# Turning an encoder's input with two engines and widening its first group of products, in one fused float32 kernel

## The chip, the cores and the metric

The kernel runs on one core of a Trainium2 chip. The metric is the device time of one execution in microseconds (us); the figure given for a kernel is the median of its runs. An engine is called by its name or by the profile's short form: TensorE (PE, with PEld for its weight loads), VectorE (DVE), ScalarE (ACT), GpSimd (POOL) and SyncE (SP, which here only issues transfers).

## What is computed

One layer of an encoder, for 256 prompt rows and 32 sample rows of 2048 features, all in float32. The change is in the first two lines; the rest follows them.

```python
xn   = rmsnorm(x, norm_mix_pre)              # x * rsqrt(mean(x*x) + eps) * g
proj = xn @ w_in                             # 2048 -> 5664 columns: u_pool 1024 | z 2048 | xBC 2560 | dt 32
pool = pool_mixer(u_pool)                    # trailing means, then a small product per group
ssd  = ssd_mixer(z, xBC, dt)                 # causal conv, chunked scan, gate, grouped norm
x    = x + rmsnorm(concat[pool, ssd] @ w_out, norm_mix_post)
x    = x + rmsnorm(conv_ffn(rmsnorm(x, norm_ffn_pre)), norm_ffn_post)
```

The new histories and states of the pooling, the convolutions and the scan are outputs too.

## The kernel before

**Tiles.** The 256 + 32 rows are the 288 columns of every product. A tile is 128 features by 288 rows; `xn` has 16 of them (`KD`). Weights stand still in TensorE, 128x128 at a time, and the tile streams past. A float32 product is made of three: each operand is split into a high half and a rest (`hi`, `lo`, type float32r), and `mm3` (L163 to L165) adds hi·hi, hi·lo and lo·hi into one accumulator. ScalarE copies the high half (`whi`, L146; `xn`, L120) and VectorE subtracts (`wlo`, L147; `xn`, L121).

**Projections.** `project` computes some output tiles of 128 columns each over all 16 feature tiles. `fetch_w` loads weights on SP's queue into four buffers (`raw`), `split_w` splits them, and the products accumulate in one of five PSUM banks (`acc_ps`). Three more banks (`aux_ps`) serve everything else. A scheduler in the compiler orders each engine's instructions by priority and its own estimate of time; what goes through `tc.keep_in_program_order` stays in the order of the source.

**The start.** The input arrives with rows on the partitions and has to be turned, features on the partitions. The first call of `project` computes four output tiles (B and C of the scan, 256 columns each) and a narrow one (dt, 32 columns, both halves side by side, `split_narrow`, L158 and L159, products L185 and L186): 16 x 4 x 3 + 32 = 224 products. Its hook `input_tiles` loads 2 or 4 feature tiles, and TensorE turns each of them with three transposes into an auxiliary bank (L299, L300, L301); ScalarE and VectorE split the result into `xn`, with the norm's gain as a scale, and VectorE copies it unscaled (`xT`, L304) for a later residual sum. ACT's queue stores `xT` to DRAM. The last hook first turns the other parameters (`columns`, L281; `ptf`, L325).

**The sums of squares.** Behind the group, ScalarE squares the untransposed rows in three instructions (L348, L349). The square root (L351) and the reciprocal are taken on 128x3 numbers, TensorE spreads them over the partitions (L355), and a copy (L359) makes `rstd`, 128x288. Every eviction of a projection multiplies by `rstd` (`conv_in`, L380 and L381, into one of four `ebuf` buffers).

**What follows.** The next projections are eight pairs of xs tiles (96 products each), then z, the pooling input, w_out and the feed-forward weights. Between them VectorE works on the convolutions, the dt chain and the scan's masks, and TensorE multiplies quads of heads (`ssd_quad`, `py`, L562 to L568). SP's queue carries weights, blocks of transposed tiles (`blocks_out`, whose tile has one buffer) and reads of what was stored.

**Other instructions that the steps below use.** VectorE's copy at L239 repeats a small selector from SBUF to SBUF; GpSimd clears four buffers at L245; L618 is the reciprocal of another norm, on 128x288, and `psum_t` (L611) its sum on TensorE.

Of the kernel before, what the change touches and what calls it, by code (L numbers as in the profile page):

```python
# [8 lines left out]
F32 = mybir.dt.float32  # L9
# [32 lines left out]
TAIL = NT - P  # L42


@with_exitstack
def body(
# [79 lines left out]
    ahead = [0]  # L126

    def fetch_w(view, kb, nk, c0, nc_):
        raw = wpool.tile([P, nk, nc_], F32, tag="raw", name="raw")
        with tc.high_priority(offset=ahead[0]):  # L130
            sp.dma_start(out=raw, in_=view[:, kb : kb + nk, c0 : c0 + nc_])
        return raw
# [18 lines left out]
    def split_narrow(raw, kb, nk, nc_, after):  # L151

        both = xin.tile([P, nk, 2, nc_], F32R, tag="both", bufs=2, name="both")
        with ExitStack() as order:
            order.enter_context(tc.high_priority(offset=ahead[0]))
            for ins in after:
                order.enter_context(tc.issue_after(ins.ins))
            act.activation(both[:, :, 0, :], raw, AF.Copy)  # L158
            dve.tensor_tensor(both[:, :, 1, :], raw, both[:, :, 0, :].bitcast(F32), op=ALU.subtract)  # L159
        return [(kb + k, both[:, k, :, :].rearrange("p r c -> p (r c)")) for k in range(nk)]  # L160

    def mm3(out, wh, wl, a, start, stop):
        pe.matmul(out, wh, a[:, 0, :], start=start, stop=False)  # L163
        pe.matmul(out, wh, a[:, 1, :], start=False, stop=False)  # L164
        pe.matmul(out, wl, a[:, 0, :], start=False, stop=stop)  # L165

    def project(view, groups, acts, ksplit, before=None, done=None, spare=(), hold=(), behind=None):
# [7 lines left out]
        for i, (kb, n) in enumerate(ksplit):  # L175
# [5 lines left out]
            for raw, (c0, w) in zip(raws, groups):  # L181
                if w < P:
                    for k, both in split_narrow(raw, kb, n, w, after or ()):
                        o = accs[m0][: 2 * w, :]
                        pe.matmul(o, both, acts[k][:, 0, :], start=k == k_first, stop=False)  # L185
                        pe.matmul(o, both, acts[k][:, 1, :], start=False, stop=k == k_last)  # L186
                    continue
                parts = split_w(raw, kb, n, w, ((after or ()) if m0 else ()) + (hold if i else ()))
# [24 lines left out]

    ident = const.tile([P, P], F32, name="ident")
    make_identity(nc, ident)
    ones = const.tile([P, P], F32, name="ones")
    pool.memset(ones, 1.0)
# [7 lines left out]
    tc.keep_in_program_order(act.activation(warm, eps_t, AF.Copy))  # L225
# [22 lines left out]
    start = ExitStack()  # L248
    xin = start.enter_context(tc.tile_pool(name="xin", bufs=1))

    g0_in = xin.tile([KD, P], F32, name="g0_in")
    act.dma_start(out=g0_in, in_=rows(norm_mix_pre))
# [5 lines left out]
    xt = xin.tile([P, 2, D_MODEL], F32, name="xt")  # L258
    xs_ = xin.tile([NS, D_MODEL], F32, name="xs_")
    xpv = x_prompt.rearrange("o (b p) d -> p (o b) d", p=P)  # L260
# [17 lines left out]
    def columns(src, n, name):  # L278
        o = const.tile([P, n], F32, name=name)
        p_ = aux([P, n], "pt")  # L280
        pe.transpose(p_, src, ident[:n, :n])  # L281
        dve.tensor_copy(o, p_)
        return o

    g_mix_pre = columns(g0_in, KD, "g0")


    xn = []
    xT = xin.tile([P, KD, NT], F32, name="xT")
    xT_d = dram.tile([P, KD, NT], F32, name="xT_d")  # L290

    def input_tiles(kb, n):
        c = slice(kb * P, (kb + n) * P)
        sp.dma_start(out=xt[:, :, c], in_=xpv[:, :, c])
        sp.dma_start(out=xs_[:, c], in_=x_sample[0][:, c])
        for t in range(kb, kb + n):
            p_ = aux([P, NT], "pt")
            c = slice(t * P, (t + 1) * P)
            pe.transpose(p_[:, 0:P], xt[:, 0, c], ident)  # L299
            pe.transpose(p_[:, P:NP_], xt[:, 1, c], ident)  # L300
            pe.transpose(p_[:, NP_:NT], xs_[:, c], ident[:NS, :NS])  # L301
            a = atile("xn")
            last = split_from(a, p_, g_mix_pre[:, t : t + 1])
            dve.tensor_copy(xT[:, t, :], p_)  # L304
            xn.append(a)
        act.dma_start(out=xT_d[:, kb : kb + n, :], in_=xT[:, kb : kb + n, :])
        return last

    def parameters():
        pb = columns(pb_in, 108, "pb")  # L310
        g_mix_post = pb[:, 60:76]
        g_ffn_pre = pb[:, 76:92]
        g_ffn_post = pb[:, 92:108]
        pa = columns(pa_in, 124, "pa")
        pah = const.tile([P, 100], F32, name="pah")
        act.activation(pah, pa[:, 0:100], AF.Copy, scale=0.5)
        p_scale = pa[:, 100:108]
        g_ssd = const.tile([P, NX], F32, name="g_ssd")
        act.activation(g_ssd, pa[:, 108:124], AF.Copy, scale=0.5)
        pc = columns(pc_in, 120, "pc")  # L320
        pf = const.tile([P, 6, NF * 2], F32, name="pf")
        for i in range(0, 6, 3):
            p_ = aux([P, 3, NF * 2], "ptf")
            for j in range(3):
                pe.transpose(p_[:, j, :], pf_in[:, i + j, :], ident[: NF * 2, : NF * 2])  # L325
# [896 lines left out]
```

## Time and profile before

| what | value |
|---|---|
| median of 3 runs | 1353.92 us (1353.91 to 1354.41) |
| the profiled execution's own time | 1354.27 us |
| its span, first to last instruction | 1352.6 us |
| TensorE's mean granted clock | 0.999 |
| bytes moved | 252.13 MB, 186 GB/s over the span |

The span is 1.67 us shorter than the execution's own time, which holds what lies around it. A group of instructions is told by line, engine, operation and tile, with the busy time and the mean duration; "start us, us" in a timeline are start and duration from the span's beginning, and matmuls overlap, so that the distance of two starts says more than a duration. In a table of waits the columns after the colon are the total, the number and the longest. In brackets stands how long the engine was idle just before an instruction, and what ended it. VectorE is busy 38.9 of the first 57 us, and 30.8, 30.1, 31.3 and 28.7 us in the stretches from 68, 101, 135 and 169 us (33 or 34 us each).

### The profile page before, as it was taken

How to read it: one execution, taken by the hardware profiler on the slowest of the kernel's cores; microseconds unless marked ns; L12 is line 12 of the kernel's file. 1: busy time of each engine (PE TensorE's matmuls, PEld its weight loads, DVE VectorE, ACT ScalarE, POOL GpSimd, SP SyncE). 2: the span in 40 equal slices, each digit the busy share in tenths (PEclk: the TensorE clock that was granted, in tenths of full speed). 3: DMA queues.
4: the chain of work that ended last, by engine and by line, in shares of the span. 5: the costliest groups of instructions: out<-in, count | busy, mean ns of one | idle time of the engine just before them, and what ended most of it. 6: DMA issues, size and time to landing. Idle time of an engine off the chain costs nothing.

```text
span 1352.6 us, 25723 instructions
## 1 busy us (share of the span) xinstructions
PE 1340.1 (99%) x10199; PEld 1327.7 (98%) x10199; DVE 886.6 (66%) x1519; ACT 669.5 (50%) x1003; POOL 233.2 (17%) x394
## 2 busy tenths in 40 slices
PE   8999999999999999999999999999999999999997
PEld 7999999999999999999999999999999999999997
DVE  6898988779644479977676644335666666664454
ACT  6557767446534455645444433334444444454443
POOL 3132112222223320211121100001111111101110
PEclk9999999999999999999999999999999999999999
DMA  8869985464756546876545545554554554576663
GB/s 269 250 192 280 257 249 167 154 221 151 243 179 201 159 132 191 239 196 182 183 156 163 173 144 169 172 179 156 175 168 156 175 169 156 170 232 181 191 182 94
DMA packets 300135, 252.13 MB, mean 186 GB/s; under 512 B 75728, under 2 KB 293050, under 8 KB 299886
## 3 DMA queue, kind: packets, MB, share of 16 engines
q1 hardware_dynamic: 296942, 243.46, 59.0%
q0 software_dynamic: 2320, 4.65, 1.2%
q10 hardware_dynamic: 752, 2.37, 0.5%
q8 instruction: 80, 1.31, 0.4%
q14 instruction: 41, 0.34, 0.1%
HBM read 236.13 MB, written 14.31 MB: 185 GB/s over the span
## 4 chain that ended last, share of the span: by engine, by line
PE 99%; DVE 0%; DMA 0%; ACT 0%; issue 0%; DVEq 0%
PE acc L163 31%; PE acc L165 31%; PE acc L164 31%; PE pst L852 1%; PE py L562 1%; PE acc L1128 1%; PE acc_x L164 0%; PE acc_x L163 0%; PE acc_x L165 0%; PE py L564 0%; DMA xt<-in_x_prompt 0%; PE pt L299 0%; PE acc L1129 0%; PE pt L301 0%; DVE wlo L147 0%; PE acc L186 0%
## 5 line engine op out<-in xcount | busy, mean ns | idle before, releaser
L147 DVE TENSOR_TENSOR wlo<-raw,whi 128x1024 fp32r<-128x1024 f32 (+1 forms) x416 | 493.3, 1188 | 347.9 <-ACT whi L146 346.6
L146 ACT ACTIVATE whi<-raw 128x1024 fp32r<-128x1024 f32 (+1 forms) x416 | 426.6, 1028 | 498.0 <-PE acc L164 421.0
L163 PE MATMUL acc<-hn,whi 128*128 128x288 f32 x1376 | 404.1, 295 | 0.0
L164 PE MATMUL acc<-hn,whi 128*128 128x288 f32 x1376 | 403.6, 294 | 0.3 <-DVE hn L911 0.3
L165 PE MATMUL acc<-hn,wlo 128*128 128x288 f32 x1376 | 403.1, 294 | 0.0
L164 PEld LDWEIGHTS acc<-hn,whi 128*128 128x128 f32 x1376 | 259.7, 189 | 0.7 <-DVE hn L911 0.7
L165 PEld LDWEIGHTS acc<-hn,wlo 128*128 128x128 f32 x1376 | 259.6, 189 | 0.0
L163 PEld LDWEIGHTS acc<-hn,whi 128*128 128x128 f32 x1376 | 257.2, 187 | 0.1
L163 PE MATMUL acc<-xn,whi 128*128 128x288 f32 x704 | 209.3, 299 | 0.0
L164 PE MATMUL acc<-xn,whi 128*128 128x288 f32 x704 | 208.0, 296 | 0.0
L165 PE MATMUL acc<-xn,wlo 128*128 128x288 f32 x704 | 207.2, 296 | 0.0
L163 PE MATMUL acc<-fa,whi 128*128 128x288 f32 x682 | 201.9, 296 | 0.0
L164 PE MATMUL acc<-fa,whi 128*128 128x288 f32 x682 | 201.9, 296 | 0.0
L165 PE MATMUL acc<-fa,wlo 128*128 128x288 f32 x682 | 201.5, 295 | 0.0
L164 PEld LDWEIGHTS acc<-xn,whi 128*128 128x128 f32 x704 | 133.6, 190 | 0.3
L165 PEld LDWEIGHTS acc<-xn,wlo 128*128 128x128 f32 x704 | 132.9, 189 | 0.3
L163 PEld LDWEIGHTS acc<-xn,whi 128*128 128x128 f32 x704 | 132.4, 189 | 0.5
L164 PEld LDWEIGHTS acc<-fa,whi 128*128 128x128 f32 x682 | 128.6, 188 | 0.0
L163 PEld LDWEIGHTS acc<-fa,whi 128*128 128x128 f32 x682 | 128.1, 188 | 0.0
L165 PEld LDWEIGHTS acc<-fa,wlo 128*128 128x128 f32 x682 | 127.9, 188 | 0.0
L945 POOL COPY fc_stage<-ebuf 128x4 f32<-128x4 f32 x88 | 27.8, 316 | 503.6 <-DVE ebuf L944 460.2
L951 DVE SCALAR_TENSOR_TENSOR fc<-ebuf,pf,fc 128x290 f32<-128x290 f32 x176 | 90.4, 517 | 3.1 <-ACT fc L949 0.5
(341 smaller groups left out, 1660.7 us busy)
## 6 DMA issues: line engine op xcount, KB each, us to landing
raw<-in_w_up SPq DMA_DIRECT2D x80, 1024.0 KB, 5.2
raw<-in_w_in SPq DMA_DIRECT2D x40, 1024.0 KB, 5.7
raw<-in_w_down SPq DMA_DIRECT2D x32, 1024.0 KB, 5.3
raw<-in_w_out SPq DMA_DIRECT2D x24, 1024.0 KB, 5.6
raw<-in_w_down SPq DMA_DIRECT2D x16, 768.0 KB, 5.0
raw<-in_w_up SPq DMA_DIRECT2D x14, 512.0 KB, 4.1
gb<-g_d SPq DMA_DIRECT2D x8, 832.0 KB, 5.4
raw<-in_w_in SPq DMA_DIRECT2D x6, 512.0 KB, 6.0
```

The source lines that it names most:

```text
L146: act.activation(hi, raw[:, k : k + n, :], AF.Copy)
L147: dve.tensor_tensor(lo, raw[:, k : k + n, :], hi.bitcast(F32), op=ALU.subtract)
L163: pe.matmul(out, wh, a[:, 0, :], start=start, stop=False)
L164: pe.matmul(out, wh, a[:, 1, :], start=False, stop=False)
L165: pe.matmul(out, wl, a[:, 0, :], start=False, stop=stop)
L562: ins = pe.matmul(y[c, 0:256], xw[:, 0, f_], m[:, h, 0:256], start=True, stop=False)
L852: ins = pe.matmul(st[:, o, :], x_, btok[:, gi, b, :], start=b != 1, stop=b != 0)
L945: pool.tensor_copy(fc_stage[:, :, :, i], e[:, 256:324].rearrange("p (s c) -> p s c", c=34)[:, :, 0:2])
L951: dve.scalar_tensor_tensor(c, e[:, r_ : r_ + 290], pf[:, r_, i : i + 1], c, op0=ALU.mult, op1=ALU.add)
L1128: pin(pe.matmul(o, hi, f2[k][:, :, c], start=k == 0, stop=end, skip_group_check=True))
```

## The change

The first group now computes six output tiles and dt: the four of B and C and the first pair of xs, whose own call of `project` goes (the pair's banks are two of the three auxiliary ones). It runs over ten chunks of features: four of one tile, six of two. The first four tiles (512 features) are still turned by TensorE, from a load of their own (`x0`, `x0s`), and the turn of the next one is placed at the tenth product of a chunk. The other twelve are loaded so that each group of 32 partitions holds another 128 features of 32 rows, and VectorE transposes them in blocks of 32. For that, features beyond 512 go to partitions in fours (`p j`), in the weights' rows, the gain and the stored `xT` alike; `fetch_w` reads `w_in` in two transfers. Fifteen dummy products (`keep_busy`) are put before the real ones; their operand `busy` is made by three VectorE copies of `ones`. Squares are taken chunk by chunk on ScalarE; GpSimd and TensorE bring them together, and root and reciprocal are now taken on 128x288. The parameters' PSUM copies go from VectorE to ScalarE, `xT`'s stores from ACT's queue to SP's, one per tile, behind the second xs pair's loads. Nearly all of the group is pinned in program order.

```diff
+CHUNKS = ((0, 1), (1, 1), (2, 1), (3, 1), (4, 2), (6, 2), (8, 2), (10, 2), (12, 2), (14, 2))
+BUSY = 10
...
+            if len(view.shape) == 4:
+                for k in range(kb, kb + nk, 4):
+                    src = view[:, k // 4] if k else win0
+                    sp.dma_start(out=raw[:, k - kb : k - kb + 4, :], in_=src[:, :, c0 : c0 + nc_])
...
+    busy = xin.tile([P, NT], F32R, name="busy")
+    for o, n in BLK:
+        pin(dve.tensor_copy(busy[:, o : o + n], ones[:, 0:n]))
...
+    win = w_in.rearrange("o (c p j) w -> p (o c) j w", p=P, j=4)
+    win0 = w_in[0, 0 : 4 * P, :].rearrange("(k p) w -> p k w", p=P)
...
+    def input_load(c):
+        for i in range(4):
+            pin(sp.dma_start(out=xt[NS * i : NS * (i + 1), 0:8, c - 1, :], in_=xpv[i][:, :, c, :]))
+
+    def first_load(kb, n):
+
+        raw = wpool.tile([P, n, NW], F32, tag="raw", name="raw")
+        src = win0[:, kb : kb + n] if kb < 4 else win[:, kb // 4, kb % 4 : kb % 4 + n]
+        pin(sp.dma_start(out=raw[:, :, 2 * P :], in_=src[:, :, O_B : O_B + NW - 2 * P]))
+        pin(sp.dma_start(out=raw[:, :, : 2 * P], in_=src[:, :, O_X : O_X + 2 * P]))
+        raws.append(raw)
...
+    pin(act.dma_start(out=g_in, in_=norm_mix_pre[0, 0 : 4 * P].rearrange("(k p) -> k p", p=P)))
+    first_input(sp, 0, 0)
+    first_input(act, 1, 0)
+    pin(act.dma_start(out=x0s, in_=x_sample[0, :, 0 : 4 * P]))
+    first_load(*CHUNKS[0])
+    first_input(sp, 0, 1)
+    first_input(sp, 1, 1)
+    first_load(*CHUNKS[1])
+    first_load(*CHUNKS[2])
+    first_load(*CHUNKS[3])
+    input_load(1)
...
-    def input_tiles(kb, n):
-        c = slice(kb * P, (kb + n) * P)
-        sp.dma_start(out=xt[:, :, c], in_=xpv[:, :, c])
-        sp.dma_start(out=xs_[:, c], in_=x_sample[0][:, c])
-        for t in range(kb, kb + n):
...
-        act.dma_start(out=xT_d[:, kb : kb + n, :], in_=xT[:, kb : kb + n, :])
...
+    first = [aux([P, NT], "acc_x") for _ in range(2)]
+    first += [acc_ps.tile([P, NT], F32, tag="acc", name="acc") for _ in range(5)]
+
+    def keep_busy(n):
+
+        for _ in range(n):
+            pin(pe.matmul(first[1], busy[:, 0:P], busy, start=True, stop=True))
+
+    keep_busy(BUSY)
...
+    def turn_first(t):
+        p_ = aux([P, NT], "pt")
+        for b in range(2):
+            pin(pe.transpose(p_[:, b * P : (b + 1) * P], x0[:, b, t * P : (t + 1) * P], ident))
+        pin(pe.transpose(p_[:, NP_:], x0s[:, t * P : (t + 1) * P], ident[:NS, :NS]))
+        return p_
+
+    def prepare(i, p_=None):
...
+        w = xin.tile([P, n, 2 * NW + HEADS], F32R, tag="w", bufs=3, name="w")
...
+        if i == 0:
+            pin(act.activation(xn[0][:, 0, :], p_, AF.Copy, scale=g_mix_pre[:, 0:1]))
+        for c in pieces:
+            pin(act.activation(hi[:, :, c], raw[:, :, c], AF.Copy))
+        pin(act.activation(w[:, :, 2 * NW :], raw[:, :, NB:], AF.Copy))
+        for t in tiles:
+            if p_ is None:
+                pin(dve.transpose(
+                    xT[t].rearrange("p (b t) -> p b t", t=NS),
+                    xt[:, :, t // 4 - 1, :].rearrange("p b (f j) -> p b f j", j=4)[:, :, :, t % 4],
+                ))
...
+        if p_ is None:
+            for c in pieces:
+                pin(dve.tensor_tensor(lo[:, :, c], raw[:, :, c], hi[:, :, c].bitcast(F32), op=ALU.subtract))
+        for t in tiles:
+            pin(dve.scalar_tensor_tensor(
+                xn[t][:, 1, :], xT[t] if p_ is None else p_, g_mix_pre[:, t : t + 1], xn[t][:, 0, :].bitcast(F32),
+                op0=ALU.mult, op1=ALU.subtract,
+            ))
+        if p_ is not None:
+            pin(dve.tensor_copy(xT[kb], p_))
+            for c in pieces:
+                pin(dve.tensor_tensor(lo[:, :, c], raw[:, :, c], hi[:, :, c].bitcast(F32), op=ALU.subtract))
+        if i + 4 < len(CHUNKS):
+            first_load(*CHUNKS[i + 4])
...
+    p_ = turn_first(0)
+    keep_busy(5)
+    ahead_w = [prepare(0, p_)]
+    for i, (kb, n) in enumerate(CHUNKS):
+        if 4 <= i + 1 < len(CHUNKS):
+            ahead_w.append(prepare(i + 1))
...
+        if i == len(CHUNKS) - 1:
+
+            pool.tensor_tensor(
+                spots, ssum[:, :9].unsqueeze(2).broadcast_to([P, 9, NS]), sel4.unsqueeze(1).broadcast_to([P, 9, NS]),
+                op=ALU.mult,
+            )
...
+            last_split[:] = [
+                pin(act.activation(rstd, p_, AF.Sqrt, bias=eps_t, scale=1.0 / D_MODEL)),
+                pin(dve.reciprocal(rstd, rstd)),
+            ]
+        w = ahead_w.pop(0)
+
+        products = [
+            (r, m, k, x) for m in (2, 3, 4, 5, 0, 1) for k in range(n) for r, x in ((0, 0), (0, 1), (1, 0))
+        ]
+        if i == 0:
+            products.sort(key=lambda q: (q[0], q[3]))
+        products += [(None, 6, k, x) for k in range(n) for x in range(2)]
+        for q, (r, m, k, x) in enumerate(products):
+            if q == 10 and i < 3:
+                ahead_w.append(prepare(i + 1, turn_first(i + 1)))
...
+    xs_ps = [first[:2], project(win, [(O_X + 256, 256)], xn, K16, wait=last_split)]
+    xT_f = xT_d.rearrange("c p j n -> (c p j) n")
+    for t in range(KD):
+        pin(sp.dma_start(out=xT_d[t // 4, :, t % 4, :] if t > 3 else xT_f[t * P : (t + 1) * P, :], in_=xT[t]))
```

Here `NB` is 768 and `NW` 800 columns, the six tiles and dt.

231 lines of the change are left out of this document (128 added, 103 removed).

## The prediction

> **What bounds the kernel now.** I read the page's busy times first. TensorE has work for 99% of the span, so the time is the sum of its instructions and its waits, and an edit counts only by what it takes from or adds to that line.
>
> ```profile
> PE 1340.1 (99%) x10199; PEld 1327.7 (98%) x10199; DVE 886.6 (66%) x1519; ACT 669.5 (50%) x1003; POOL 233.2 (17%) x394
> ```
>
> TensorE's waits come next: 5.2 of the 6.6 us lie before 7 us; none lies between 42 and 300 us.
>
> ```profile
> PE pt L281 <- DMA g_in<-in_norm_mix_pre: 3.4, 1, 3.4
> PE pt L299 <- DVE xT L304: 1.5, 1, 1.5
> PE psum_f L1050 <- ACT fsq L1173: 1.1, 1, 1.1
> ```
>
> Then TensorE's timeline: start, duration, line. A product is issued each 0.24 us until 12.4 us, and each 0.132 us later (37 between 57.04 and 61.93). The clock column shows 1.00 in both stretches, so I take the clock from this spacing. A turned input tile is a hole: from 24.37 to 25.09 there are three transposes and one product, 0.59 us more than the product. Other holes cost 0.54 to 0.59; I use 0.58.
>
> ```profile
> 4.02 0.48 PE L299 MATMUL pt<-ident,xt 128*128 128x128 f32 x1 [0.34 <-DMA xt<-in_x_prompt]
> ...
> 7.27 0.83 PE L163 MATMUL acc<-xn,whi 128*128 128x288 f32 x2
> ...
> 10.17 0.68 PE L163 MATMUL acc<-xn,whi 128*128 128x288 f32 x2
> ...
> 24.37 0.27 PE L299 MATMUL pt<-ident,xt 128*128 128x128 f32 x1
> 24.48 0.27 PE L300 MATMUL pt<-ident,xt 128*128 128x128 f32 x1
> 24.68 0.24 PE L301 MATMUL pt<-ident,xs__137 32*128 32x32 f32 x1
> 24.86 0.40 PE L163 MATMUL acc<-xn,whi 128*128 128x288 f32 x1
> ```
>
> **The yardstick.** The new first group computes 320 products: the old group's 224 and the 96 of the first xs pair. I compare when these 320 are issued. Before: the first 28 are out at 14.24 us; 292 x 0.132 = 38.5; eleven tiles still to turn, 6.4; the end of one more, 0.2; parameter transposes (0.11 + 0.11 + 0.39 + 0.27), 0.9; L355, 0.95. Sum **61.2 us**. As a check, 180 products stand ahead of L355, which gives 41.8; the trace has it at 41.95.
>
> **After, step by step.** The last operand sets each step, so I read the loads' arrivals from ACT's timeline (the bracket tells what ended ACT's idle time).
>
> ```profile
> 6.09 0.63 ACT L146 ACTIVATE whi<-raw 128x512 fp32r<-128x512 f32 x1 [0.18 <-DMA raw<-in_w_in]
> ...
> 7.70 0.63 ACT L146 ACTIVATE whi<-raw 128x512 fp32r<-128x512 f32 x1 [0.59 <-DMA raw<-in_w_in]
> ...
> 10.62 0.63 ACT L146 ACTIVATE whi<-raw 128x512 fp32r<-128x512 f32 x1 [0.44 <-DMA raw<-in_w_in]
> ```
>
> By the kernel's sizes, 550, 1060 and 1900 KB were queued up to these three loads.
>
> *First product.* Chunk 0's first weight piece ends at 590 KB: about 6.0 us. ACT copies 544 columns in 0.65, so the first product is at 6.7 (7.27 before). The fifteen added dummy products lie where TensorE waits for loads; ones' memset ends at 1.02, three VectorE copies of some 0.2 each make the dummy operand by 1.7, and ten products at 0.24 end at 4.1, where the first input lands. If the clock is up by 8 us the chunk's 20 products end at 9.9.
>
> *Chunk 1.* Its weights end at 1380 KB: 8.8 us between the rows of 7.70 and 10.62, which are also the bounds. ACT: 800 columns 0.85, dt columns 0.15, split 0.45: 10.3. DVE in its pinned order: low half 0.43, copy 0.37, then the weights' low half (800 columns, 0.98 between the 0.69 of 512 and the 1.21 of 1024), with 0.1 of handovers: **12.2 us**. Chunk 1's third product needs that. A chunk 0 still at half speed is mostly hidden in this wait; it would move it to 12.4.
>
> *Chunks 2 and 3.* The tile is turned at the tenth product of the chunk before, and one auxiliary bank is left for it. From the turn: 0.55 + 0.5 (ACT) + 0.43 + 0.37 + 0.98 + 0.2 handovers = 3.03. TensorE meanwhile has 0.58 + 12 x 0.132 = 2.16. Wait 0.85 each.
>
> *Chunk 4.* VectorE starts its blocks after chunk 3's low half: two transposes (0.39 start to start in the blocks rows), 1600 columns 1.75, low half 0.43, handover 0.1: 3.1 against 2.5 of products. Wait 0.6. The trace has no strided block transpose: at nothing more than a plain row, or twice it, this wait is 0.6 to 1.4; I take 0.6, the same element count.
>
> *Chunks 5 to 9.* VectorE needs 0.78 + 1.75 + 0.86 = 3.4 per chunk, ACT 2.6 (4.0 with three squares), TensorE 40 x 0.132 = 5.3. A chunk brings 1.1 MB (weights 820 KB, input 290), 208 GB/s over 5.3 us; the first two slices of the page moved 269 and 250. So block transposes, squares, input loads and SP's extra issues (0.45 us each, 39 of them, 17.6 us of the 57) lie under products; if loads fell to 200 GB/s they would cost 0.2 us per chunk. The 16 stores of xT (7.2 us of issue) move from ACT's queue to SP's, between weight loads that go out a buffer release, some 10 us, ahead of use; their tiles are done, so they hold nothing up.
>
> *End of the group.* Parameters 0.9; sums 0.48 (a 288-column psum_t) + 0.95 (as L355) = 1.4. Then the new wait: the next product needs a bank, since all five accumulators are taken. The reciprocal is now on 128x288 and the rows price it:
>
> ```profile
> L618 DVE RECIPROCAL rg<-rg 128x288 f32<-128x288 f32 x2 | 3.9, 1948 | 0.6 <-ACT rg L617 0.6
> ```
>
> Behind it on VectorE stand two weight halves (2 x 1.1) and the evictions. From the sums' end: 0.55 + 1.95 + 2.2 + 0.34 + 0.34 + 0.2 = 5.6, against 5.3 of products: wait 0.4. ACT's table load lies ahead of the sums. POOL's product for the sums (1.1 to 1.4 us by its 128x288 rows) has a chunk of cover.
>
> Sum: 12.2 + 298 x 0.132 (39.3) + two turns 1.2 + 1.7 + 0.6 + 0.9 + 1.4 + 0.4 = **57.7 us**, a gain of 3.5. From some 290 us on every compute engine's order in the changed build is as before, so I carry the gain through. Profiled execution: 1354.27 (span 1352.6 and 1.67 around it) - 3.5 = 1350.8; the median of the runs shown, 1353.92, is 0.35 lower: **1350.4**.
>
> **Rivals.**
>
> *A. The dummy operand is late (1351.9).* The dummy products need VectorE copies from SBUF to SBUF, pinned ahead of all else on TensorE. The trace has one such copy beside GpSimd work:
>
> ```profile
> 1.80 2.08 DVE L239 COPY sel<-sel 32x128 f32<-32x128 f32 x1
> ```
>
> ```profile
> 2.52 1.28 POOL L245 MEMSET ebuf<- 128x326 f32 x4
> ```
>
> 128 columns take 2.08 us and end with the last memset (3.80). If the three new copies wait likewise, dummies run from 4.25 to 6.7, the turn ends at 7.6, the split and weights give a first product at 8.85, chunk 1's low half comes at 13.3 to 14.1: 1.1 to 1.9 lost, 1351.9 in the middle. Against it, and why I don't take it as likeliest: GpSimd pauses at 1.23, just after the new copies are asked for at 1.05 (ones' memset ends at 1.02 in the new order), where the old copy came at 1.80 into an unbroken row of memsets. *SBUF — State Buffer* (the Trainium skill, Who interferes with whom) says that a Vector copy in a two-port mode and a GpSimd operation exclude one another for a whole instruction; the copy row agrees, and by that rule this rival holds.
>
> *B. VectorE's backlog (1358.1).* Before, VectorE has done 42.7 us of work when the 320 products are out; after, about 33 (four turned tiles at 1.7, twelve others at 0.83 with 10.5 for their weights, reciprocal 1.95, two weight halves 2.2, start 1.5). So 9.7 us move behind them, where VectorE idles 14.0 us between 68 and 203, 8 of them in order behind stores. If less than 6.2 us of the idle is usable the gain is gone; with 2 usable the kernel is 4.2 slower. Against it: ACT waited there for weight buffers, so the splits ran ahead.
>
> *C. Chunk 1's weights land at the later row (1352.2).* 10.6 instead of 8.8: 1.8 less gain, since the chain behind them stays. For it: each transfer is queued behind the input. Against it: fewer bytes stand ahead than at that row.
>
> *D. The small waits shrink (1348.0).* Chunk 1 lands at the earlier row, 1.1 sooner, and half of the waits of 1.7 + 0.6 + 0.4 is covered, 1.35: 2.4 more. For it: weight packets of 2176 bytes replace 1024. Against it: VectorE's chain per chunk is as long either way.
>
> *TensorE: Matmul & The Clock Gate* (the Trainium skill, Part 1) states a busy window of 3.4 us before full speed, free-running. By it the dummies would raise the clock between 5 and 8.5 us; the spacing row, 5.4 us after 6.96, allows that. The sum by 12.4 us instead is 0.2 worse.
>
> **How the numbers follow.** What can be told from no change is 0.2%, 2.7 us: faster is under 1351.2, slower over 1356.6. Forecast 0.40 (0.36 of it faster), A 0.24 (0.04 faster), B 0.16 (0.12 slower), C 0.08 (same), D 0.12 (faster). Faster 0.52, same 0.36, slower 0.12. The range holds forecast, A, C and D and leaves out B: from D, 1348.0, to A's dear end (1.9) with the dear strided transpose (0.8) and slow loads (1.0), 1354.1.
>
> **What would show it.** First product near 6.7, or near 8.9 with the first dummy after 4 us (A). Waits for the weights' low half in chunks 1 to 3, near 12.2 and twice 0.85. One wait of the product after the group on VectorE's eviction. No TensorE wait between 60 and 300 us, or B. Wrong altogether if chunks 5 to 9 wait for loads, or if the spacing after 13 us isn't 0.132.

## The result, and the profile after

The changed kernel takes **1359.05 us** (median of 11 runs, 1355.02 to 1362.12) where the kernel before takes 1353.93 (11 runs beside it, 1353.36 to 1354.49): a ratio of 1.0034, 95% interval 1.0022 to 1.0046. It is 0.34% slower, outside the range and on the other side of the forecast. The profiled execution is one of the longer ones: 1361.21 us, a span of 1359.3, against 1354.27 and 1352.6 before. So 6.9 us are to be found in the traces, and 5.1 in the medians.

The first line of the changed kernel's page, busy times and instructions:

```profile
PE 1342.0 (99%) x10180; PEld 1328.6 (98%) x10180; DVE 889.6 (65%) x1509; ACT 672.6 (49%) x1028; POOL 235.4 (17%) x395
```

VectorE as a whole does 3.0 us more than before; nothing here tells of trouble. TensorE's table of waits does:

```profile
PE psum_t L740 <- POOL gsum L762: 3.8, 1, 3.8
PE acc L475 <- DVE w L397: 1.9, 3, 0.6
PE acc_x L337 <- DVE busy L213: 1.7, 1, 1.7
PE acc L164 <- DVE wlo L157: 1.6, 3, 0.8
```

The second and third lines lie in the start and were forecast. The first and the fourth are new, and lie between 187 and 238 us, where the kernel before has no wait: rival B's place. `psum_t` is TensorE's sum over the partitions of the squares of the first gated half; GpSimd adds these squares (`gsum`) as VectorE hands over the gated tiles. Two rows of TensorE's timeline (start, duration, idle time before it) show the waits, and the table by stretch beneath (TensorE busy, its instructions, the granted clock, the DMA share, GB/s) what follows the longer one:

```profile
187.55 0.40 PE L164 MATMUL acc<-xn,wlo 128*128 128x288 f32 x1 [0.80 <-DVE wlo L157]
...
237.51 1.33 PE L740 MATMUL psum_t<-gsum,ones 128*128 128x288 f32 x2 [3.75 <-POOL gsum L762]
```

```profile
235.00:237.00 2.00, 0.00 (x0) 0.70 0.00 0
237.00:239.00 2.00, 1.49 (x4) 0.50 0.41 78
239.00:241.00 2.00, 2.00 (x10) 0.50 1.08 377
241.00:243.00 2.00, 2.00 (x12) 0.59 0.91 239
243.00:245.00 2.00, 2.00 (x17) 1.00 1.03 353
```

After 3.75 us without work the granted clock is 0.50, and products are issued each 0.24 us until 242.6 instead of each 0.132. *TensorE: Matmul & The Clock Gate* (the Trainium skill, Part 1) says that an idle window of about 3.4 us halves the clock and a busy one restores it; this trace agrees, with 3.75 us of idle time and 5.1 us until it was back. Other runs do not need so long a wait: 1.88 us was enough in `e11` and 3.18 us not enough in `e1` (the last section compares them). The runs of the changed kernel differ in it: five of the 11 have a mean clock of 0.998 or 0.999 and take 1355.0 to 1359.1 us, six 0.996 or 0.997 and take 1358.4 to 1362.1.

**Where the 6.9 us arise.** I compare both traces where TensorE has issued equally many products of the projections. At product 1088 the changed kernel is ahead by 2.0 us (171.61 against 173.58). By the quad at product 1376 1.7 of these are gone, with two waits for `wlo` of 0.80 and 0.26 in between. Each wait sets the products behind it back by some 0.27 us more than TensorE is idle, since matmuls overlap (0.80 by 1.07, 0.26 by 0.53). Up to `psum_t` it loses 4.8 more, in waits of 0.57 and 3.75; the half-speed stretch costs 2.4. From there on the distance stays, to the end: -2.0 + 1.7 + 4.8 + 2.4 = 6.9.

**VectorE's list.** The last thing that VectorE does for that sum is the eighth multiplication of `xs` by `z` (L651, after: L780). It ends at 225.26 us before and at 235.66 after. The table by stretch from zero to that point, for before and for after (length; busy time and instructions of PE, PEld, DVE, ACT, POOL; clock; DMA share; GB/s):

```profile
0.00:225.26 225.26, 220.02 (x1712) 212.32 (x1713) 190.71 (x381) 147.20 (x270) 54.09 (x102) 1.00 0.83 242
```

```profile
0.00:235.66 235.66, 227.27 (x1751) 218.75 (x1751) 197.00 (x374) 153.98 (x298) 56.19 (x103) 1.00 0.83 234
```

VectorE is 10.4 us later: 6.3 of work and 4.1 of idle time. By lines, the added work is mainly: turning and splitting the input 15.9 instead of 13.4 (block transposes 7.2, low halves 7.2, copies 1.5; before, low halves 7.6 and copies 5.8); the reciprocal on 128x288 in place of a copy, +1.5; low halves of weights, +1.0; one product `m` (an operand of the quads) more ahead of it in the list, +1.6; the dummy operand +0.6; the parameters' copies -1.4. The idle time contains 5.5 us that was not there:

```profile
54.32 1.95 DVE L451 RECIPROCAL rstd<-rstd 128x288 f32<-128x288 f32 x1 [5.47 <-ACT rstd L450]
```

VectorE stands ahead of the reciprocal, whose sums come at the group's end, and the next splits are held behind it. In the kernel before, the last addition to `gsum` ended at 227.9, 2.6 us ahead of `psum_t` at 230.52; that was all the slack there was:

```profile
226.42 1.45 POOL L633 TENSOR_TENSOR gsum<-gsum,sq 128x288 f32<-128x288 f32 x1 [3.66 <-ACT sq L632]
...
230.52 0.65 PE L611 MATMUL psum_t<-gsum,ones 128*128 128x288 f32 x2
```

After, it ends at 237.46:

```profile
236.35 1.11 POOL L762 TENSOR_TENSOR gsum<-gsum,sq 128x288 f32<-128x288 f32 x1 [0.99 <-ACT sq L761]
```

Divided where product 320 is issued (61.5 before, 59.4 after), VectorE's table (length, busy time and instructions, clock, DMA share, GB/s) reads, before and after:

```profile
0.00:61.50 61.50, 43.40 (x87) 1.00 0.87 264
61.50:225.26 163.76, 147.31 (x295) 1.00 0.82 234
```

```profile
0.00:59.40 59.40, 38.06 (x58) 1.00 0.98 269
59.40:235.66 176.26, 158.94 (x317) 1.00 0.78 222
```

So 5.3 us of VectorE's work moved behind the group and 6.3 us are new; its idle time behind the group is 17.3 us where it was 16.5, so none of it took in the 11.6 us.

### The profile page after: what moved, and what is told of

It reads as the page before. It is cut to its first block, busy times and chain, and to the rows that moved or that the text cites. A ratio compares the mean times of both kernels' runs of the same rounds, so it can differ in the third digit from the quotient of the medians.

```text
span 1359.3 us, 25801 instructions
## 1 busy us (share of the span) xinstructions
PE 1342.0 (99%) x10180; PEld 1328.6 (98%) x10180; DVE 889.6 (65%) x1509; ACT 672.6 (49%) x1028; POOL 235.4 (17%) x395
## 4 chain that ended last, share of the span: by engine, by line
PE 91%; DMA 4%; DVE 2%; SPq 1%; issue 1%; ACT 1%; POOL 0%; DVEq 0%; ACTq 0%; POOLq 0%
PE acc L162 29%; PE acc L164 29%; PE acc L163 28%; DMA xs_d<-blocks 2%; DMA raw<-in_w_in 1%; PE acc L475 1%; PE pst L980 1%; SPq L202 1%; PE acc L1255 1%; DVE wlo L157 1%; PE acc_x L475 0%; DMA xt<-in_x_prompt 0%; DMA xk<-xs_d 0%; DVE m L679 0%; PE py L691 0%
## 5 line engine op out<-in xcount | busy, mean ns | idle before, releaser
L157 DVE TENSOR_TENSOR wlo<-raw,whi 128x1024 fp32r<-128x1024 f32 (+1 forms) x402 | 479.8, 1195 | 342.1 <-ACT whi L156 341.0
L156 ACT ACTIVATE whi<-raw 128x1024 fp32r<-128x1024 f32 (+1 forms) x402 | 413.5, 1031 | 481.6 <-PE acc L163 401.6
L164 PE MATMUL acc<-xn,wlo 128*128 128x288 f32 x608 | 179.7, 296 | 1.6 <-DVE wlo L157 1.6
L162 PE MATMUL acc<-xn,whi 128*128 128x288 f32 x608 | 181.1, 298 | 0.2 <-DVE ebuf L506 0.2
L163 PE MATMUL acc<-xn,whi 128*128 128x288 f32 x608 | 180.6, 297 | 0.0
L164 PEld LDWEIGHTS acc<-xn,wlo 128*128 128x128 f32 x608 | 115.5, 190 | 2.6 <-DVE wlo L157 2.3
L163 PEld LDWEIGHTS acc<-xn,whi 128*128 128x128 f32 x608 | 115.7, 190 | 0.3
L162 PEld LDWEIGHTS acc<-xn,whi 128*128 128x128 f32 x608 | 114.7, 189 | 0.8 <-issue 0.4
L1068 POOL COPY ebuf<-pf 128x2 f32<-128x2 f32 x88 | 72.0, 818 | 129.6 <-DVE fc L1079 58.9
```

The costliest lines, as they stand in the source:

```text
L156: act.activation(hi, raw[:, k : k + n, :], AF.Copy)
L157: dve.tensor_tensor(lo, raw[:, k : k + n, :], hi.bitcast(F32), op=ALU.subtract)
L162: then(pe.matmul(out, wh, a[:, 0, :], start=start, stop=False))
L163: then(pe.matmul(out, wh, a[:, 1, :], start=False, stop=False))
L164: then(pe.matmul(out, wl, a[:, 0, :], start=False, stop=stop))
L1068: pool.tensor_copy(e[:, 258:260], pf[:, 4:6, i])
```

## The experiments

Theory 1: VectorE's list ahead of the first gate sum is longer and starts later, has no slack left, and TensorE waits for it. Its rivals: SyncE's longer queue (2), the planner's other order with its stops for DMAs (4, 6). In the table, "done" is the end of that eighth multiplication, "stops" the part of VectorE's idle time that waits for the blocks stored to `xs_d` or for the loads of `xk` that read them back, "waits" TensorE's between 62 and 300 us, all from the profiled execution; times are medians, the ratio is that of the means to the kernel before in the same runs, so that it can differ a little from the medians'.

| kernel | done | work | idle | stops | waits | us | ratio, 95% |
|---|---|---|---|---|---|---|---|
| before | 225.3 | 190.7 | 34.6 | 11.8 | 0 | 1353.93 | |
| after | 235.7 | 197.0 | 38.7 | 10.9 | 5.4 | 1359.05 | 1.0034 (1.0022 to 1.0046) |
| e1_four_tiles | 229.2 | 193.7 | 35.5 | 12.4 | 3.2 | 1361.5 | 1.0055 (1.0042 to 1.0068) |
| e2_sp_longer | 226.1 | 191.1 | 35.0 | 13.2 | 0.2 | 1353.82 | 0.9998 (0.9990 to 1.0007) |
| e3_sum_later | 234.1 | 197.2 | 36.9 | 11.6 | 3.0 | 1353.87 | 1.0003 (0.9995 to 1.0011) |
| e5_dose4 | 229.7 | 197.5 | 32.1 | 11.2 | 0.8 | 1355.88 | 1.0015 (1.0007 to 1.0024) |
| e6_dose8 | 249.2 | 208.0 | 41.2 | 20.6 | 11.1 | 1368.58 | 1.0113 (1.0099 to 1.0127) |
| e7_splits_free | 227.3 | 194.1 | 33.2 | 11.0 | 1.4 | 1356.10 | 1.0014 (1.0005 to 1.0023) |
| e8_free_and_later | 225.5 | 194.4 | 31.1 | 9.1 | 0 | 1353.89 | 1.0003 (0.9994 to 1.0012) |
| e9_four_early | 228.7 | 194.5 | 34.2 | 10.2 | 1.9 | 1356.24 | 1.0013 (1.0004 to 1.0022) |
| e10_sorted | 226.6 | 194.6 | 32.0 | 8.2 | 0 | 1355.00 | 1.0001 (0.9992 to 1.0010) |
| e11_sorted_only | 232.1 | 197.2 | 34.9 | 8.7 | 1.9 | 1357.65 | 1.0024 (1.0014 to 1.0034) |
| e12_before_later | 223.3 | 191.1 | 32.3 | 8.8 | 0 | 1354.25 | 1.0001 (0.9992 to 1.0010) |
| e13_third_late | 231.0 | 197.2 | 33.8 | 10.1 | 2.4 | 1352.40 | 0.9985 (0.9975 to 0.9995) |
| e15_third_late_free | 227.6 | 194.4 | 33.1 | 9.8 | 1.7 | 1353.97 | 1.0001 (0.9993 to 1.0010) |
| e16_two_taps | 227.6 | 185.5 | 42.1 | 11.2 | 2.8 | 1355.16 | 1.0009 (1.0000 to 1.0018) |
| e17_two_blocks | 234.7 | 198.0 | 36.7 | 12.3 | 5.8 | 1361.09 | 1.0050 (1.0036 to 1.0064) |
| e18_two_blocks_best | 230.4 | 198.0 | 32.4 | 11.2 | 2.7 | 1356.24 | 1.0020 (1.0011 to 1.0029) |
| e19_before_two_blocks | 228.2 | 192.2 | 36.1 | 11.9 | 3.7 | 1358.21 | 1.0028 (1.0019 to 1.0038) |

### Parts of the change: the group's width, SyncE's queue

`e1`, on the changed kernel:

```diff
-NB = 768
+NB = 512
...
-    first = [aux([P, NT], "acc_x") for _ in range(2)]
-    first += [acc_ps.tile([P, NT], F32, tag="acc", name="acc") for _ in range(5)]
+    first = [acc_ps.tile([P, NT], F32, tag="acc", name="acc") for _ in range(5)]
...
-    xs_ps = [first[:2], project(win, [(O_X + 256, 256)], xn, K16, wait=last_split)]
+    xs_ps = [project(win, [(O_X, 256)], xn, K16, wait=last_split)]
```

> The changed kernel with its first group narrowed to four output tiles and dt: the first pair of xs tiles is a projection of its own again, as before the change; the turned input and the spread squares stay. Theory 1 (the six-tile group hands dt and B/C to VectorE some 12 to 15 us later, and what VectorE owes is not caught up by the first gate sum): the wait of TensorE for the last gsum addition (3.8 us in the changed kernel) and the wlo waits between 180 and 235 us shrink to the kernel before's, time 1352 to 1355. Theory 2 (SyncE's queue, longer by the weights loaded in two transfers and the stores of xT by tile, holds up the xs_d stores and xk loads): the waits stay, time 1358 to 1360.

1361.5 us. The wait for `gsum` did go, but one of 3.18 us for `wlo` came at 195.6, behind stops of VectorE of 5.2 and 2.2 us for `xk`. The profiled execution, at 1358.18 us, is the fastest of the six and has the highest mean clock (0.999, the others 0.994 to 0.997). So theory 1's first form, that the six-tile group is to blame for the late list, falls; with four tiles VectorE still has 3.0 us more work than before, and TensorE still waits.

`e2`, on the kernel before:

```diff
-            sp.dma_start(out=raw, in_=view[:, kb : kb + nk, c0 : c0 + nc_])
+            step = 4 if view is win and nk == 8 else nk
+            for k in range(0, nk, step):
+                sp.dma_start(out=raw[:, k : k + step, :], in_=view[:, kb + k : kb + k + step, c0 : c0 + nc_])
...
-        act.dma_start(out=xT_d[:, kb : kb + n, :], in_=xT[:, kb : kb + n, :])
...
+    for t in range(KD):
+        sp.dma_start(out=xT_d[:, t, :], in_=xT[:, t, :])
```

> The kernel before with only SyncE's part of the change: the weights of w_in in two transfers of four k-tiles each, and the 16 stores of xT issued one by one by SyncE. Theory 1: nothing on TensorE's path waits for SyncE, 1353 to 1355, with psum_t waiting under 0.5 us for gsum. Theory 2: xs_d stores and xk loads come later, VectorE's chain with them, TensorE waits some 3 to 4 us for gsum, 1357 to 1360.

1353.82 us, a wait of 0.2. SyncE's added transfers cost nothing: theory 2 falls.

`e4` put the third weight block into the first group of the kernel before:

```diff
-        win, [(O_B, 256), (O_C, 256), (O_DT, HEADS)], xn, ...
+        win, [(O_B, 256), (O_C, 256), (O_X, 256), (O_DT, HEADS)], xn, ...
+        spare=[aux([P, NT], "acc_x") for _ in range(2)],
...
-    xs_ps = [project(win, [(O_X, 256)], xn, K16)]
+    xs_ps = [first[4:6]]
```

> The kernel before with only the wider first group: its three weight blocks are B, C and the first xs pair, then dt, over the input turned on TensorE as before; one projection less follows. Theory 1: dt, B and C come some 10 us later, the wait for gsum and some waits for wlo appear around 180 to 235 us without the turned input, and the time is 1356 to 1361. Theory 2: no such waits, since SyncE issues what it issued before; the start alone changes, by 2 us at most either way, 1352 to 1356.

1383.16 us, 1.0210 (1.0197 to 1.0223), far outside both. With one auxiliary bank left, TensorE's turning stalls (VectorE idles 23.5 us for `xn`), so the start swamps what was asked. It decides nothing between the theories.

### The place of the sum

`e3` on the changed kernel, `e12` the same on the kernel before:

```diff
-        if i == 4:
+        if i == 5:
             assert gates[0] >= 8
             rg.append(rstd_all(gsum[0], 0.25 / 1024, "rg0"))
-        if i > 4:
-            for t in range(3 * i - 15, min(8, 3 * i - 12)):
+        if i > 5:
+            for t in range(4 * i - 24, 4 * i - 20):
```

> The changed kernel with the first gate's sum of squares (the product of ones with gsum) placed one pair of z tiles later, and the multiplications by its result four and four instead of three, three, two. Theory 1: by then GpSimd's addition has long ended, the 3.8 us wait and the 2.4 us that the products after it lost at half pace both go, time 1351.5 to 1354, and the runs lie within 1 us of each other. Theory 2 (SyncE's lateness is the cause, and the sum only where it first shows): the lateness shows at the next thing that needs VectorE, time within 1.5 us of the changed kernel's 1359.

> The kernel before with the first gate sum one pair of z tiles later. Theory 1: there the addition was 2.6 us ahead of the sum already, so a later place gains nothing: 1353.2 to 1354.8. If a later place were a gain by itself: 1352.5 or less.

`e3`: 1353.87 us, 5.2 below the changed kernel, with no wait for `gsum` and the mean clock at 0.999 or 1.000 in 11 of 12 runs. `e12`: 1354.25, no gain. So the later place takes the wait away where there is one and is worth nothing by itself. Of `e3`'s forecast the median came true; the narrow spread did not (1351.98 to 1358.38), since 3.0 us of waits for `wlo` stay: VectorE is late whatever TensorE asks it for.

### More and less work on VectorE

`e5` and `e6`, on the kernel before, with 4 and 8 repetitions:

```diff
-    dve.tensor_copy(rstd, p_)
+    with tc.high_priority(offset=400):
+        tc.keep_in_program_order(dve.tensor_copy(rstd, p_))
+        for i in range(4):
+            tc.keep_in_program_order(
+                dve.tensor_tensor(dose, xf[:, 1024 * (i % 4) : 1024 * (i % 4 + 1)], xf[:, 0:1024], op=ALU.subtract)
+            )
```

> The kernel before with 4 added subtractions of 128x1024 on VectorE right behind rstd's copy (some 1.2 us each, 4.8 in all; nothing reads their result). Theory 1 (VectorE's work ahead of the first gate sum is the limit): the last gsum addition ended at 227.9 us in the kernel before, 2.6 ahead of TensorE's sum at 230.5; 4.8 us more work makes it some 2 us late, time 1355 to 1357.5. Theory 4 (VectorE has 34.5 us of idle time ahead of that addition, and it is the other order of instructions, with its waits for the loads of xk, that costs): the idle time takes the added work in, time within 1 us of 1353.9.

> The kernel before with 8 such subtractions, 9.6 us of added VectorE work. Theory 1: the last gsum addition is some 7 us late, a wait of that size on TensorE, and products at half pace behind it as in the changed kernel, time 1361 to 1366. Theory 4: the idle time takes it in, time within 1.5 us of 1353.9.

1355.88 us with a wait of 0.75 for `gsum`, and 1368.58 with 11.1 us of waits behind 62 us, none of which the kernel before has. The unchanged kernel thus shows the changed kernel's illness when VectorE alone gets more to do behind `rstd`. Four subtractions (4.5 us) cost 1.9 us, as forecast, of which the traces put 1.0 at the gate sum, 0.4 at a wait for `wlo` at 222 and 0.5 ahead of 162. Eight cost 14.6, more than forecast and more than they last: in that list the stops nearly doubled as well (20.6 us), and of the 11.1 us only 2.1 are for `gsum`; 4.5 are for a quad's operand (`xw`) at 180. So `e5` bears out the direction and the place; `e6` bears out the direction alone.

`e16`, on the changed kernel, does the opposite:

```diff
-        for r in range(1, 4):
+        for r in range(1, 3):
             dve.scalar_tensor_tensor(
```

> The changed kernel with two of the convolution's three VectorE taps; the third, 0.43 us for each of 20 tiles, is left out, 8.6 us of VectorE work ahead of the first gate sum. Nothing else is changed. Theory 1 (the sum of VectorE's work and idle time ahead of that sum is what TensorE waits for): VectorE is done ahead of TensorE, no wait for gsum or wlo between 60 and 240 us, half pace nowhere behind 12 us, and the start's 2 us arrive at the end: 1351 to 1353. Theory 4 (waits of VectorE for the loads of xk and state, in its order): those waits take up the freed time, TensorE still waits over 1.5 us for gsum, 1355 to 1358.

1355.16 us: 3.9 less than the changed kernel. The wait for `gsum` is gone and the list is done 8.1 us sooner, as theory 1 says; the time is theory 4's, since a wait of 2.27 us for `wlo` stands at 189.6 and 11.5 us less work brought 3.4 us more idle time. VectorE's timeline (start, duration, idle time before) shows what it waits behind:

```profile
187.95 0.48 DVE L199 STREAM_TRANSPOSE blocks<-xs 128x288 f32<-128x288 f32 x1 [3.28 <-DMA xs_d<-blocks]
188.35 1.18 DVE L157 TENSOR_TENSOR wlo<-raw,whi 128x1024 fp32r<-128x1024 f32 x1
```

The split that TensorE needs stands behind a transpose that has to wait for its one buffer to be stored. Work is not all.

### Using VectorE's idle time ahead of the reciprocal

`e7` on the changed kernel, `e8` on `e3`:

```diff
-    xs_ps = [first[:2], project(win, [(O_X + 256, 256)], xn, K16, wait=last_split)]
+    xs_ps = [first[:2], project(win, [(O_X + 256, 256)], xn, K16)]
```

> The changed kernel without the rule that keeps the splits of the second xs pair's weights behind the reciprocal of rstd (the argument wait of that call). Theory 1: VectorE, idle for 5.5 us ahead of the reciprocal and more before it, does up to four splits of 1.15 us there, its later work comes 3 to 4.6 us sooner, and the wait for gsum falls from 3.8 to under 1 us: time 1353 to 1355.5. Theory 4: the waits for the xk loads stay as they are, time 1357.5 to 1360.

> Both at once: the splits free as in the last kernel, and the first gate sum one pair of z tiles later. Theory 1: neither that wait nor the ones for wlo between 185 and 236 us are left, and the early gain of some 2 us and a little more is kept: 1350.5 to 1352.5, runs within 2 us of each other. Theory 4: waits for wlo behind xk stay, 1353 to 1356.

`e7`: 1356.10 us, the list done 8.4 us sooner, the wait for `gsum` 1.4. That is theory 1's direction, 0.6 us above its range. `e8`: no TensorE wait at all between 62 and 300 us, yet 1353.89. Its start is part of the reason: ScalarE splits the early weights ahead of the parameters' copies, TensorE waits 2.5 us for these, and the next projection starts at 60.4 instead of 59.4 (61.5 in the kernel before). The profiled execution keeps this gain of 1.1 us to the end (a span of 1351.3 against 1352.6); why the median does not, one trace can't show.

`e9` holds the splits behind the last of those copies instead (`last_split` is set there), on `e3`:

```diff
-                pin(act.activation(pf[:, q // 8 : q // 8 + 3, :], p_, AF.Copy))
+                last_split[:] = [pin(act.activation(pf[:, q // 8 : q // 8 + 3, :], p_, AF.Copy))]
...
-            last_split[:] = [
-                pin(act.activation(rstd, p_, AF.Sqrt, bias=eps_t, scale=1.0 / D_MODEL)),
-                pin(dve.reciprocal(rstd, rstd)),
-            ]
+            pin(act.activation(rstd, p_, AF.Sqrt, bias=eps_t, scale=1.0 / D_MODEL))
+            pin(dve.reciprocal(rstd, rstd))
```

> The first gate sum one pair of z tiles later, and the splits of the second xs pair held only behind the last copy of the parameters (pf) on ScalarE instead of behind the reciprocal: four splits then stand right ahead of the reciprocal, and none ahead of the parameters' copies, whose lateness cost 2.5 us of waits when nothing held the splits. Theory 1: the start is the changed kernel's (the next projection's first product near 59.4, 2 us ahead of the kernel before), no wait for wlo or gsum between 60 and 300 us, the 2 us arrive at the end: 1350.5 to 1352.5. Theory 4 (the waits of VectorE for xk loads go on costing TensorE): 1353 to 1356.

1356.24 us, a miss for both theories. The next projection's first product comes at 58.9, but waits of 1.9 us are back (1.27 at 221.7), and VectorE idles 5.2 us for loads of state beside 10.2 us of stops. Each new list puts its stops elsewhere, and I could not tell beforehand where.

### The start

`e11` on the changed kernel, `e10` on `e9`:

```diff
-        if i == 0:
+        if i < 5:
             products.sort(key=lambda q: (q[0], q[3]))
```

> The changed kernel with the products of chunks 1 to 4 sorted and nothing else. Theory 1: TensorE and VectorE's reciprocal both come up to 2 us sooner, VectorE's list behind it is the same, so the wait for gsum stays at 3 to 4 us with half pace behind it, and the time falls by at most those 2 us: 1356.5 to 1359. If a faster start alone settled it: 1353 or less.

> The last kernel with the products of chunks 1 to 4 sorted as those of chunk 0 are: first all with the weights' and the input's high halves, then those with the input's low half, then those with the weights' low half. Twelve products, 1.6 us, then stand ahead of the first that needs the weights' low half, where two stood. Theory 1: the four waits of 0.56 to 0.63 us go, and since VectorE is no longer what TensorE waits for later, the gain arrives: 1.5 to 2.4 us below the last kernel. Rival: the time between chunks is set by VectorE's and ScalarE's chains per chunk, the waits only move, within 0.8 us of the last kernel.

`e11` 1357.65 us, as theory 1 had it; `e10` 1355.00, 1.2 below its base, between the two forecasts. The waits of chunks 1 to 4 (2.4 us) went, and one of 2.8 us came at 34.9. ScalarE's and TensorE's timelines of `e11`:

```profile
30.40 1.54 ACT L374 ACTIVATE w<-raw 128x1600 fp32r<-128x1600 f32 x1 [5.02 <-DMA raw<-in_w_in]
```

```profile
34.94 0.33 PE L320 MATMUL pt<-ident,pa_in 124*128 124x124 f32 x1 [2.79 <-ACT pb L426]
```

The weights of chunk 6 are late, ScalarE with them, and the parameters' copy stands behind. Behind this wait the clock is 0.50 for another 3.4 us. So the loads bound the start as soon as the small waits are gone.

`e13` (on `e3` with sorted products) and `e15` (on `e10`) ask for the third part of the input later:

```diff
         if i == 1:
             input_load(2)
-            input_load(3)
+        if i == 3:
+            input_load(3)
...
-    SQUARES = {6: range(3), 7: range(3, 6), 8: range(6, 9)}
+    SQUARES = {7: range(4), 8: range(4, 9)}
```

> The changed kernel with the gate sum one pair later and sorted products in chunks 1 to 4, and the third part of the turned input (features 1536 to 2047, 4 transfers) asked for two chunks later; the squares, which need it, go to chunks 7 and 8. In the kernels with sorted products the weights of chunk 6 landed at 30.4 us, behind 8 input loads that SyncE took 8 us to issue, and TensorE waited 2.7 us two instructions on. Theory L (the loads' order bounds the start): those weights land 2 to 4 us sooner, the wait goes, and the start is 1.5 to 2.4 us faster than the changed kernel's: 1350 to 1352.5. Rival (the 16 DMA engines are full between 10 and 30 us, and order only moves the wait to a later chunk): 1353 to 1355.

> The same two edits of loads and squares on the kernel that has sorted products, the later gate sum and four splits ahead of the reciprocal (1355.0 us). Theory L: its 2.7 us wait goes, 1351 to 1353.5. Rival: 1354 to 1356.

`e13`: **1352.40 us**, 0.9985 (0.9975 to 0.9995), inside theory L's range and the only kernel whose interval lies below the kernel before, though by less than the 0.2% that the prediction counts as no change. Those weights land at 28.4 instead of 30.4, TensorE waits 0.2 us between 8 and 62 us, and the next projection starts at 56.7. `e15`: 1353.97, 1.0 below `e10`, between the two forecasts. With sorted products alone it started at 60.2 (`e11`), so the order of the loads (with the squares that follow it) was worth 3.4 us there, the half-speed stretch behind the wait included, although the DMA engines were full (a share above 1.0 from 10 to 30 us in `e11`). In its profiled execution (1354.30 us, one of the longer ones of 1349.28 to 1355.38) the gain is lost again: `e13` is 4.8 us ahead of the kernel before at product 320 and level with it at the end, after waits for `wlo` of 0.55 at 188 and 1.89 at 232 and a clock of 0.50 for 3.4 us behind the second.

### A second buffer for the blocks

`e17` on the changed kernel, `e18` on `e13`, `e19` on the kernel before:

```diff
-        s = pool_.tile([P, NT], F32, tag="blocks", bufs=1, name="blocks")
+        s = pool_.tile([P, NT], F32, tag="blocks", bufs=2 if pool_ is mp else 1, name="blocks")
```

> The changed kernel with two buffers instead of one for the turned blocks that go out to xs_d (in the mixer's pool; nothing else is edited). In the run with two taps VectorE had 11.5 us less work done by the first gate sum and yet idled 3.3 us for the stores of one such buffer, and TensorE 2.3 us behind it. Theory 6 (the changed kernel's later list leaves no slack, and it is the stops for that buffer and for xk, not the work as such, that turn into TensorE waits): VectorE's idle time for the stores of blocks (4.9 us ahead of the gate sum) goes, the wait for gsum falls by 2 us or more: 1354 to 1357. Theory 1 in its strict form (work alone): the wait stays within 1 us of 3.8, 1358 to 1360.

> The fastest kernel so far (gate sum one pair later, sorted products, third part of the input later; 1352.4 us) with two buffers for the blocks. Theory 6: its waits for wlo at 188 and 232 us (0.6 and 1.9) shrink to under 1 us together, 1349.5 to 1351.5. Theory 1 strict: within 1 us of 1352.4.

> The kernel before with two buffers for the blocks, as a control: its VectorE idled 11.0 us for those stores, but TensorE had no wait between 42 and 300 us, so both theories say no gain: 1353 to 1354.5.

1361.09, 1356.24 and 1358.21 us: no gain anywhere, and losses of 3.8 us for `e13` and 4.3 for the kernel before, which no theory had. VectorE's waits between 60 and 235 us, for the changed kernel and for `e17`:

```profile
DVE xw L668 <- DMA xk<-xs_d: 6.0, 4, 2.6
DVE blocks L199 <- DMA xs_d<-blocks: 4.9, 4, 1.9
```

```profile
DVE xw L668 <- DMA xk<-xs_d: 12.3, 5, 3.9
```

The stop for the buffer is gone and the one for the read-back has grown by as much: 10.9 became 12.3 us. The blocks go to DRAM and come back, and VectorE waits for this round trip at one end or the other; in all kernels of the table but `e6` the stops sum to 8.2 to 13.2 us. Theory 6, as I wrote it, falls; and `e17`'s unchanged wait of 3.7 us is what theory 1 in its strict form said. In `e19` VectorE's list is done only 3.0 us later, but a stop of 4.1 us for `xk` now stands four instructions ahead of a split that TensorE needs: a wait of 2.9 us at 195.5.

## Why the prediction was wrong

**The failing step** is "From some 290 us on every compute engine's order in the changed build is as before, so I carry the gain through". It was the step from a local gain to the end of the kernel. Between 60 and 290 us TensorE meets VectorE, and VectorE was 10.4 us later with 2.6 us of slack. Equal order from 290 us on says only that a loss before it is kept, too. The sum has no term for what VectorE owes further behind the group: neither for the 5.3 us moved there nor for the 6.3 us added.

**Rival B was what happened,** with 1358.1 us for a measured 1359.05. Its mechanism, VectorE's backlog that TensorE meets before 300 us, holds (`e5`, `e7`, `e3` with its control `e12`). That its number came so near is luck: it moved 9.7 us and found 2 us of idle time usable, and 5.3 us moved, 6.3 were added and none was usable; the half-speed stretch of 2.4 us it did not have. My ground against it was that the splits ran ahead; after the change they did not (waits of 0.80, 0.26 and 0.57 for `wlo`), and the longest wait hangs on the gated tiles. I gave it a chance of 0.16 and left it outside the range. What I should have read off was the slack at the one fixed meeting: the last `gsum` row against the `psum_t` row.

**The early gain was 2.0 us, not 3.5.** The first product came at 7.61, not 6.7: the sample rows landed at 5.95 and the turn waited for them. Chunk 1's low half came at 13.23, forecast 12.2, and not by its weights, which landed at 8.16: its turned tile stood behind ten products at half pace, so that ScalarE's split started at 10.86. The two waits of 0.85 were 0.63 and 0.61, the one of 0.6 was 0.56 although its block transposes took 0.61 and not the assumed 0.39, the one of 0.4 behind the group was 0.18, and chunks 5 to 9 had none over 0.1, as forecast. But each wait costs some 0.27 us more than its idle time, about 1.1 us for the first four, which the sum leaves out. That the loads lie under products held only because TensorE was late itself; with 2.4 us less waiting they did not (`e11`).

**The clock did not come up between 5 and 8.5 us.** Products came each 0.24 us until 10.0, and the granted clock is first recorded, at 1.00, at 10.5. With the same dummies it came at 5.2 in four other runs and between 9.1 and 12.4 in the rest.

**The dummy operand (A) was not late:** three casts ended 0.55 us after their start at 1.05, beside GpSimd's memsets. The selector's copy, which A took as its row, still ended with the last memset (3.89); why the casts did not is not shown. C did not happen: chunk 1's weights landed at 8.16, not 10.6.

**What stays open.** How much each part of the added work weighs was not separated. Nor is it settled why the lists of `e9`, `e18` and `e19` put their stops where TensorE feels them: every edit makes the planner write a new list, and its times are not those of the chip. In `e16`, `e18` and `e19` stops of 3.3, 4.6 and 4.1 us stand ahead of the late split, so theory 4 is not excluded as a part. Differences of 2 to 4 us between lists remain that I do not explain.

## What to carry to other kernels

Before carrying a gain of the bound engine to the end, find the next fixed place where it needs another engine, and compare that engine's list up to there (work and idle time) with the slack at that place; idle time is not free if it is a wait of its own. Here an engine that waited for a round trip through memory kept that wait when one of its buffers was doubled; it only moved. If a sum has a fixed place and its operand is late, try a later place first: it was a few lines, and it was worth 5.2 us.

## What the runs showed of the hardware that I had not expected

- A block transpose of 128x288 from a source with a stride of four elements took 0.58 to 0.63 us from start to start, 0.39 to 0.40 for the contiguous one of the kernel before.
- The length of a wait alone did not decide whether TensorE's clock halved: waits of 1.88 (`e11`), 1.89 (`e13`) and 3.75 us (the changed kernel) did it, one of 3.18 us (`e1`'s profiled execution) did not. In all 20 traces the granted clock changes only at whole steps of 3.41 us from its first record. Divided into these steps, `e13` has 1.89 us of idle time in one of them and `e1` 1.61 and 1.57 in two (length, TensorE busy, its instructions, clock, DMA share, GB/s):

```profile
229.94:233.35 3.41, 1.52 (x12) 1.00 0.02 3
233.35:236.77 3.42, 3.42 (x16) 0.50 0.94 303
```

```profile
190.66:194.07 3.41, 1.80 (x14) 1.00 0.53 145
194.07:197.49 3.42, 1.85 (x13) 1.00 0.46 70
```

  Of the 15 falls to 0.50 that the traces show before 1300 us, 13 follow a step with 1.88 us of idle time or more, over half of it; the other two (1.48 and 1.08 us) lie in `e4`'s start, among many short holes. The largest idle time of a step that left the clock at 1.00 is 1.69. No run was made to test this.
- Between 10 and 30 us the changed start's DMA engines were busy all the time (a share of 1.12 and 1.13) at 243 and 233 GB/s, where the kernel before moved 331 and 266 at 1.07 and 0.92. The input in groups of 32 partitions is loaded at a worse rate: in the changed kernel's trace of these 20 us the packets of 512 bytes, most of them its rows, moved 10 bytes per ns of their time, those of 1024 and 2176 bytes, the weights', 16 and 17. SyncE took 8.1 us in `e11` to issue eight such loads in a row, and 1.9 for the first four.
